# Rotary embedding on one core: loading the first tile as f32 on another queue, with compact constants and new rows

## The chip, the core and the metric

The kernel runs on one core of one Trainium2 chip. The metric is device time in microseconds (us), lower is better. A time in this text is the median of the runs of a kernel; the profile adds a span, which is about 2 us shorter than the time.

The data lies in HBM, the large memory; SBUF is the memory of the core, with 128 partitions. A transfer between them (DMA) is issued here by one of the engines SyncE, ScalarE and GpSimd, each with a queue of its own (136, 144 and 2304 packets in the kernel before), and carried in packets by the core's 16 DMA engines. VectorE and ScalarE compute on SBUF.

## The reference

```python
batch, n_heads, seq, head_dim = 8, 8, 1024, 64      # x is f32, 16.8 MB
angles = np.outer(positions, freqs)                 # 1024 x 32
cos, sin = np.cos(angles), np.sin(angles)
x_first, x_second = x[..., :32], x[..., 32:]
out_first  = x_first * cos - x_second * sin
out_second = x_first * sin + x_second * cos
```

The output is f32 and as large as the input. `positions` arrive as 64-bit integers.

## The kernel before

The 64 (batch, head) planes are cut into eight tiles of 128 partitions x 4096 elements. A partition holds 64 positions of one head, 16 KB of f32 in HBM. GpSimd issues all large transfers, and they cast: f32 in HBM, bf16 in SBUF, both ways. VectorE does six bf16 operations per tile.

```python
def hbm(t, g):                       # partition p takes row p of the tile: plain rows
    return bass.AP(tensor=t.tensor, offset=t.offset + g * P * run, ap=[[run, P], [1, run]])

pos_i = singles.tile([P, C, 1], positions.dtype)
nc.sync.dma_start(out=pos_i, in_=bass.AP(..., ap=[[0, group], [C, chunks], [1, C]]))
fr = singles.tile([P, half], f32)
nc.scalar.dma_start(out=fr, in_=freqs[None, :].to_broadcast([P, half]))
for g in range(ntiles):              # eight loads, f32 -> bf16
    nc.gpsimd.dma_start(out=xt..., in_=hbm(x, g))
# ... VectorE: turns = positions x freqs, range reduction; ScalarE: sin_h, cos_h (bf16)
for g in range(ntiles):
    v.tensor_mul(out=t1, in0=xf, in1=sin_h);  v.tensor_mul(out=t2, in0=xs, in1=sin_h)
    v.tensor_mul(out=of, in0=xf, in1=cos_h);  v.tensor_mul(out=os_, in0=xs, in1=cos_h)
    v.tensor_sub(out=of, in0=of, in1=t2);     v.tensor_add(out=os_, in0=os_, in1=t1)
    nc.gpsimd.dma_start(out=hbm(out, g), in_=ot...)      # store, bf16 -> f32
```

Of the kernel before, what the change touches and what calls it, by code (L numbers as in the profile page):

```python
# [2 lines left out]

# [4 lines left out]


@with_exitstack  # L10
def kernel(
    ctx: ExitStack,
    tc: tile.TileContext,
    x: bass.AP,
    freqs: bass.AP,
    positions: bass.AP,
    out: bass.AP,
):
    nc = tc.nc
    f32 = mybir.dt.float32  # L20
    bf16 = mybir.dt.bfloat16
    Sin = mybir.ActivationFunctionType.Sin
    Alu = mybir.AluOpType

    b, h, seq, d = x.shape
    bh = b * h
    half = d // 2
    P = 128
    twopi = 2 * math.pi


    C = 64
    chunks = seq // C
    group = P // chunks
    ntiles = bh // group
    run = C * d
    assert chunks * C == seq and group * chunks == P and ntiles * group == bh

    singles = ctx.enter_context(tc.tile_pool(name="singles", bufs=1))
    xpool = ctx.enter_context(tc.tile_pool(name="xin", bufs=ntiles))  # L40
    opool = ctx.enter_context(tc.tile_pool(name="xout", bufs=ntiles))
    tpool = ctx.enter_context(tc.tile_pool(name="tmp", bufs=2))

    def hbm(t, g):
        return bass.AP(tensor=t.tensor, offset=t.offset + g * P * run, ap=[[run, P], [1, run]])


    pos_i = singles.tile([P, C, 1], positions.dtype)
    nc.sync.dma_start(
        out=pos_i,  # L50
        in_=bass.AP(tensor=positions.tensor, offset=positions.offset,
                    ap=[[0, group], [C, chunks], [1, C]]))
    fr = singles.tile([P, half], f32)
    nc.scalar.dma_start(out=fr, in_=freqs[None, :].to_broadcast([P, half]))


    xts = []
    for g in range(ntiles):
        xt = xpool.tile([P, C, d], bf16)
        nc.gpsimd.dma_start(out=xt.rearrange("p c d -> p (c d)"), in_=hbm(x, g))  # L60
        xts.append(xt)


    half_pi = singles.tile([P, 1], f32)
    nc.vector.memset(half_pi, math.pi / 2)  # L65
    pos_f = singles.tile([P, C, 1], f32)
    nc.vector.tensor_copy(out=pos_f, in_=pos_i.bitcast(mybir.dt.int32)[:, :, :1])  # L67
    fturn = singles.tile([P, 1, half], f32)
    nc.vector.tensor_scalar_mul(out=fturn[:, 0, :], in0=fr, scalar1=1.0 / twopi)  # L69
    turns = singles.tile([P, C, half], f32)  # L70
    nc.vector.tensor_mul(out=turns, in0=pos_f.to_broadcast([P, C, half]),  # L71
                         in1=fturn.to_broadcast([P, C, half]))
    whole = singles.tile([P, C, half], f32)
    magic = 1.5 * 2.0 ** 23
    nc.vector.tensor_scalar(out=whole, in0=turns, scalar1=magic, scalar2=magic,  # L75
                            op0=Alu.add, op1=Alu.subtract)
    nc.vector.tensor_sub(out=turns, in0=turns, in1=whole)  # L77
    sin_h = singles.tile([P, C, half], bf16)
    cos_h = singles.tile([P, C, half], bf16)
    nc.scalar.activation(out=sin_h, in_=turns, func=Sin, scale=twopi)  # L80

    nc.scalar.activation(out=whole, in_=turns, func=mybir.ActivationFunctionType.Abs)  # L82
    nc.scalar.activation(out=cos_h, in_=whole, func=Sin, scale=-twopi, bias=half_pi)  # L83

    v = nc.vector
    for g in range(ntiles):
        xt = xts[g]
        xf = xt[:, :, :half]
        xs = xt[:, :, half:]
        ot = opool.tile([P, C, d], bf16)  # L90
        of = ot[:, :, :half]
        os_ = ot[:, :, half:]
        t1 = tpool.tile([P, C, half], bf16)
        t2 = tpool.tile([P, C, half], bf16)
        v.tensor_mul(out=t1, in0=xf, in1=sin_h)  # L95
        v.tensor_mul(out=t2, in0=xs, in1=sin_h)  # L96
        v.tensor_mul(out=of, in0=xf, in1=cos_h)  # L97
        v.tensor_mul(out=os_, in0=xs, in1=cos_h)  # L98
        v.tensor_sub(out=of, in0=of, in1=t2)  # L99
        v.tensor_add(out=os_, in0=os_, in1=t1)  # L100
        nc.gpsimd.dma_start(out=hbm(out, g), in_=ot.rearrange("p c d -> p (c d)"))  # L101


# [1 line left out]
_INS = ['x', 'freqs', 'positions']  # L105
_OUTS = [((8, 8, 1024, 64), 'float32')]


# [23 lines left out]
```

## Time and profile before

| | before |
|---|---|
| time | 86.48 us (86.31 to 86.53, 3 runs) |
| span of the profiled run | 84.2 us |
| first load packet starts / last store lands | 2.84 / 82.83 us |
| one tile's f32 side, load or store | 2.10 MB in 4.86 us, 431 GB/s |
| VectorE | 60.7 us busy, done at 67.7 us |

These are lines of the page of the kernel before: the span, the busy time of the engines, the busy tenths of VectorE and of the DMA engines in 40 slices of 2.1 us, what the DMA engines moved in each slice, and the DMA issues with KB and median us to landing.

```profile
span 84.2 us, 132 instructions
DVE 60.7 (72%) x54; ACT 7.0 (8%) x4; POOL 8.9 (11%) x20
DVE  0069927999999999999999999999999910000000
DMA  0399999999999999999999999999999999999990
GB/s 2 60 210 214 214 218 218 214 214 214 214 222 210 218 218 210 218 218 214 210 342 405 459 405 467 381 490 381 482 389 467 405 451 420 428 443 405 467 373 0
...
out_dram<-ot POOLq DMA_DIRECT2D x8, 2048.0 KB, 21.7
xt<-in_x_dram POOLq DMA_DIRECT2D x8, 1024.0 KB, 23.6
```

The DMA row is full from the third slice to the end: the kernel is a stream. The rate row counts the bytes written, so a cast load shows its bf16 side: 215 GB/s written means 430 GB/s read. Loads fill the first half and stores the second, because the stores queue behind the loads on one queue: the first store is issued at 22.6 us, and its first packet starts at 43.3 us, while the last packets of the loads end. VectorE is done when seven slices of stores are still to come.

The stages of the start, as windows (start:end, length, busy us of VectorE, ScalarE and GpSimd, TensorE clock, DMA share, GB/s written):

```profile
2.00:4.00 2.00, 0.00 (x0) 0.42 (x1) 2.00 (x5) 1.00 0.36 53
4.00:6.00 2.00, 1.04 (x3) 0.00 (x0) 1.63 (x4) 1.00 1.00 204
6.00:8.00 2.00, 1.97 (x2) 0.00 (x0) 0.00 (x0) 1.00 1.01 209
```

And from the timeline (start, duration, engine and line, what it did, in brackets what it waited for):

```profile
0.74 0.74 SPq L49 DMA_DIRECT2D pos_i<-in_positions_dram  x1
1.25 4.38 POOL L60 DMA_DIRECT2D xt<-in_x_dram  x8 [0.80 <-PEq L127]
4.93 0.20 DVE L67 CAST pos_f<-pos_i 128x64 f32<-128x64 int32 x1 [4.06 <-DMA pos_i<-in_positions_dram]
...
67.99 0.53 POOL L101 DMA_DIRECT2D out_dram<-ot  x1 [6.28 <-DVE ot L100]
```

The stream is thin until about 4.5 us. That head is what the change goes for. The last store is issued at 68.0 us, long before its turn on the queue.

### The profile page before, as it was taken

How to read it: one execution, taken by the hardware profiler on the slowest of the kernel's cores; microseconds unless marked ns; L12 is line 12 of the kernel's file. 1: busy time of each engine (PE TensorE's matmuls, PEld its weight loads, DVE VectorE, ACT ScalarE, POOL GpSimd, SP SyncE). 2: the span in 40 equal slices, each digit the busy share in tenths (PEclk: the TensorE clock that was granted, in tenths of full speed). 3: DMA queues.
4: the chain of work that ended last, by engine and by line, in shares of the span. 5: the costliest groups of instructions: out<-in, count | busy, mean ns of one | idle time of the engine just before them, and what ended most of it. 6: DMA issues, size and time to landing. Idle time of an engine off the chain costs nothing.

```text
span 84.2 us, 132 instructions
## 1 busy us (share of the span) xinstructions
DVE 60.7 (72%) x54; ACT 7.0 (8%) x4; POOL 8.9 (11%) x20
## 2 busy tenths in 40 slices
DVE  0069927999999999999999999999999910000000
ACT  4100079900000000000000000000000000000000
POOL 5960000000201100200200200100020020000000
DMA  0399999999999999999999999999999999999990
GB/s 2 60 210 214 214 218 218 214 214 214 214 222 210 218 218 210 218 218 214 210 342 405 459 405 467 381 490 381 482 389 467 405 451 420 428 443 405 467 373 0
DMA packets 2584, 25.25 MB, mean 300 GB/s; under 512 B 408, under 2 KB 536, under 8 KB 536
## 3 DMA queue, kind: packets, MB, share of 16 engines
q0 software_dynamic: 2304, 25.17, 97.2%
q1 hardware_dynamic: 136, 0.07, 0.3%
q10 hardware_dynamic: 144, 0.02, 0.1%
HBM read 16.86 MB, written 16.78 MB: 399 GB/s over the span
## 4 chain that ended last, share of the span: by engine, by line
issue 65%; DMA 10%; POOL 4%; POOLq 1%; PEldq 0%
DMA xt<-in_x_dram 10%; POOL out_dram L101 4%; POOLq L127 1%; POOLq L101 0%; PEldq L127 0%
## 5 line engine op out<-in xcount | busy, mean ns | idle before, releaser
L95 DVE TENSOR_TENSOR t<-xt,sin_h 128x2048 bf16<-128x2048 bf16 x8 | 9.8, 1224 | 2.0 <-ACT sin_h L80 2.0
L101 POOL DMA_DIRECT2D out_dram<-ot x8 | 4.3, 535 | 58.6 <-DVE ot L100 58.6
L99 DVE TENSOR_TENSOR ot<-ot,t 128x2048 bf16<-128x2048 bf16 x8 | 9.8, 1225 | 0.0
L97 DVE TENSOR_TENSOR ot<-xt,cos_h 128x2048 bf16<-128x2048 bf16 x8 | 9.8, 1224 | 0.0
L100 DVE TENSOR_TENSOR ot<-ot,t 128x2048 bf16<-128x2048 bf16 x8 | 9.8, 1224 | 0.0
L98 DVE TENSOR_TENSOR ot<-xt,cos_h 128x2048 bf16<-128x2048 bf16 x8 | 9.8, 1223 | 0.0
L96 DVE TENSOR_TENSOR t<-xt,sin_h 128x2048 bf16<-128x2048 bf16 x8 | 9.8, 1223 | 0.0
L60 POOL DMA_DIRECT2D xt<-in_x_dram x8 | 4.4, 578 | 0.8 <-PEq L127 0.8
L67 DVE CAST pos_f<-pos_i 128x64 f32<-128x64 int32 x1 | 0.2, 196 | 4.1 <-DMA pos_i<-in_positions_dram 4.1
L80 ACT ACTIVATE sin_h<-turns 128x2048 bf16<-128x2048 f32 x1 | 1.9, 1911 | 8.7 <-DVE turns L77 8.7
L77 DVE TENSOR_TENSOR turns<-turns,whole 128x2048 f32<-128x2048 f32 x1 | 2.3, 2293 | 0.0
L71 DVE TENSOR_TENSOR turns<-pos_f,fturn 128x2048 f32<-128x2048 f32 x1 | 2.3, 2291 | 0.0
L83 ACT ACTIVATE cos_h<-whole,half_pi 128x2048 bf16<-128x2048 f32 x1 | 2.0, 2003 | 0.0
L82 ACT ACTIVATE whole<-turns 128x2048 f32<-128x2048 f32 x1 | 1.9, 1896 | 0.0
L80 ACT ACT_TABLE_LOAD x1 | 1.3, 1283 | 1.1 <-PEq L116 1.1
L75 DVE TENSOR_SCALAR whole<-turns 128x2048 f32<-128x2048 f32 x1 | 1.2, 1226 | 0.0
L65 DVE MEMSET half_pi<- 128x1 f32 x1 | 0.1, 59 | 0.8 <-PEq L116 0.8
L69 DVE TENSOR_SCALAR fturn<-fr 128x32 f32<-128x32 f32 x1 | 0.2, 174 | 0.0
L116 POOL MEMSET const-float32-0.0<- 128x1 f32 x1 | 0.1, 99 | 0.2 <-issue 0.2
L116 POOL MEMSET const-bfloat16-1.0<- 128x1 bf16 x1 | 0.1, 102 | 0.0
L116 POOL MEMSET const-float32-1.0<- 128x1 f32 x1 | 0.1, 99 | 0.0
L116 POOL MEMSET const-uint8-127<- 128x1 uint8 x1 | 0.1, 99 | 0.0
## 6 DMA issues: line engine op xcount, KB each, us to landing
out_dram<-ot POOLq DMA_DIRECT2D x8, 2048.0 KB, 21.7
xt<-in_x_dram POOLq DMA_DIRECT2D x8, 1024.0 KB, 23.6
pos_i<-in_positions_dram SPq DMA_DIRECT2D x1, 64.0 KB
fr<-in_freqs_dram ACTq DMA_DIRECT2D x1, 16.0 KB, 3.6
```

Source lines behind the costliest of these rows:

```text
L60: nc.gpsimd.dma_start(out=xt.rearrange("p c d -> p (c d)"), in_=hbm(x, g))
L71: nc.vector.tensor_mul(out=turns, in0=pos_f.to_broadcast([P, C, half]), in1=fturn.to_broadcast([P, C, half]))
L77: nc.vector.tensor_sub(out=turns, in0=turns, in1=whole)
L80: nc.scalar.activation(out=sin_h, in_=turns, func=Sin, scale=twopi)
L83: nc.scalar.activation(out=cos_h, in_=whole, func=Sin, scale=-twopi, bias=half_pi)
L95: v.tensor_mul(out=t1, in0=xf, in1=sin_h)
L96: v.tensor_mul(out=t2, in0=xs, in1=sin_h)
L97: v.tensor_mul(out=of, in0=xf, in1=cos_h)
L98: v.tensor_mul(out=os_, in0=xs, in1=cos_h)
L99: v.tensor_sub(out=of, in0=of, in1=t2)
L100: v.tensor_add(out=os_, in0=os_, in1=t1)
L101: nc.gpsimd.dma_start(out=hbm(out, g), in_=ot.rearrange("p c d -> p (c d)"))
```

## The change

The intent: start the stream earlier. Tile 0 comes as f32 on SyncE's queue, which can issue at 0.74 us, and ScalarE casts it. So that the constants don't stand in the way, positions come on 16 partitions and frequencies on 4, and VectorE shuffles them within each group of 32 partitions. The rows are laid out anew, so that each group of 32 holds its own chunks of positions: partition = chunk x 8 + head. At the end SyncE waits early on all but the last store, to shorten the end.

```diff
     def hbm(t, g):
-        return bass.AP(..., ap=[[run, P], [1, run]])
+        return bass.AP(..., ap=[[run, chunks], [seq * d, group], [1, run]])
+    x0 = singles.tile([P, C, d], f32)
+    nc.sync.dma_start(out=x0.rearrange("p c d -> p (c d)"), in_=hbm(x, 0))
-    nc.sync.dma_start(out=pos_i, ...)
+    pos_i = singles.tile([P, C, words], i32)
+    nc.vector.memset(pos_i, 0)
+    nc.scalar.dma_start(out=pos_i[0:P:group].bitcast(positions.dtype),
+        in_=bass.AP(..., ap=[[C, chunks], [1, C], [1, 1]]))
     fr = singles.tile([P, half], f32)
-    nc.scalar.dma_start(out=fr, in_=freqs[None, :].to_broadcast([P, half]))
+    nc.vector.memset(fr, 0.0)
+    nc.scalar.dma_start(out=fr[0:P:32], in_=freqs[None, :].to_broadcast([P // 32, half]))
     for g in range(ntiles):
-        nc.gpsimd.dma_start(...)
+        if g:
+            nc.gpsimd.dma_start(...)
+    nc.vector.stream_shuffle(pos_i, pos_i, [i // group * group for i in range(32)])
+    nc.vector.stream_shuffle(fr, fr, [0] * 32)
 ... (sin_h and cos_h as before)
+    nc.scalar.copy(out=xts[0], in_=x0)
-    for g in range(ntiles):
+    for g in [1, 0] + list(range(2, ntiles)):
 ...
+    for done in [pos_i, fr, x0] + ots[:-1]:
+        sp.clobber_nop(outs=[sp.lower_ap(done)])
+    sp.keepalive_nop(ins=[sp.lower_ap(ots[-1])])
```

More of the change, by code (lines that the diff above doesn't have):

```diff
@@ L44, in hbm @@
     def hbm(t, g):
-        return bass.AP(tensor=t.tensor, offset=t.offset + g * P * run, ap=[[run, P], [1, run]])
-    pos_i = singles.tile([P, C, 1], positions.dtype)
-    nc.sync.dma_start(
-        out=pos_i,
+        return bass.AP(tensor=t.tensor, offset=t.offset + g * P * run,
+                       ap=[[run, chunks], [seq * d, group], [1, run]])
+    x0 = singles.tile([P, C, d], f32)
+    nc.sync.dma_start(out=x0.rearrange("p c d -> p (c d)"), in_=hbm(x, 0))
+    i32 = mybir.dt.int32
+    words = mybir.dt.size(positions.dtype) // 4
+    pos_i = singles.tile([P, C, words], i32)
+    nc.vector.memset(pos_i, 0)
+    nc.scalar.dma_start(
+        out=pos_i[0:P:group].bitcast(positions.dtype),
         in_=bass.AP(tensor=positions.tensor, offset=positions.offset,
-                    ap=[[0, group], [C, chunks], [1, C]]))
+                    ap=[[C, chunks], [1, C], [1, 1]]))
     fr = singles.tile([P, half], f32)
-    nc.scalar.dma_start(out=fr, in_=freqs[None, :].to_broadcast([P, half]))
+    nc.vector.memset(fr, 0.0)
+    nc.scalar.dma_start(out=fr[0:P:32], in_=freqs[None, :].to_broadcast([P // 32, half]))
     xts = []
@@ L59 @@
         xt = xpool.tile([P, C, d], bf16)
-        nc.gpsimd.dma_start(out=xt.rearrange("p c d -> p (c d)"), in_=hbm(x, g))
+        if g:
+            nc.gpsimd.dma_start(out=xt.rearrange("p c d -> p (c d)"), in_=hbm(x, g))
         xts.append(xt)
+    nc.vector.stream_shuffle(pos_i, pos_i, [i // group * group for i in range(32)])
+    nc.vector.stream_shuffle(fr, fr, [0] * 32)
     half_pi = singles.tile([P, 1], f32)
@@ L66 @@
     pos_f = singles.tile([P, C, 1], f32)
-    nc.vector.tensor_copy(out=pos_f, in_=pos_i.bitcast(mybir.dt.int32)[:, :, :1])
+    nc.vector.tensor_copy(out=pos_f, in_=pos_i[:, :, :1])
     fturn = singles.tile([P, 1, half], f32)
@@ L83 @@
     nc.scalar.activation(out=cos_h, in_=whole, func=Sin, scale=-twopi, bias=half_pi)
+    nc.scalar.copy(out=xts[0], in_=x0)
     v = nc.vector
-    for g in range(ntiles):
+    ots = []
+    for g in [1, 0] + list(range(2, ntiles)):
         xt = xts[g]
@@ L100 @@
         v.tensor_add(out=os_, in0=os_, in1=t1)
+        ots.append(ot)
         nc.gpsimd.dma_start(out=hbm(out, g), in_=ot.rearrange("p c d -> p (c d)"))
+    sp = nc.sync
+    for done in [pos_i, fr, x0] + ots[:-1]:
+        sp.clobber_nop(outs=[sp.lower_ap(done)])
+    sp.keepalive_nop(ins=[sp.lower_ap(ots[-1])])
 _INS = ['x', 'freqs', 'positions']
```

## The prediction

> **What bounds it now.** The DMA stream, from end to end. The row of DMA shares in 40 slices reads 9 from about 4.2 us to 82 us. Every tile is 2.10 MB on its f32 side. The semaphore arrivals in the trace space the eight load completions (9.8, 14.7, ... 43.9 us) and then the eight store completions (48.8, ... 82.8 us) by 4.86 us each: 431 GB/s of f32 side in both halves (the page's 215 GB/s for loads counts the bf16 side). 16 x 4.86 = 77.8 us, so of the span of 84.2 us only two ends are not stream: about 5.0 us before it (43.9 minus 8 x 4.86) and 1.4 us after it. [...] VectorE (60.7 us busy, 6.81 us per tile) is not the limit: it finishes at 67.7 us, the last store is issued at 68.0, but its packets start only at about 77.6, behind the older stores. That is some 8 us of slack.
>
> **What the change removes.** The empty head. GpSimd issues the first load at 1.25 us, its first packet starts at 2.8, and packets come one per 0.61 us on all engines only from about 4.5; the 264 small constant packets sit in front (1.7 to 4.6 us). In the new kernel SyncE can issue tile 0 at 0.74 us. ACT's constant load, issued at 0.74, had its first packet at 1.73; so I expect full rate from about 2.0 to 2.3 us, with GpSimd's stream joining before tile 0 runs out. The same bytes pass [...]. Gain: about 2.4 us, all on the critical path.
>
> **What it adds, off the path if the slack holds.** Two memsets and two shuffles (about 0.2 us each by the 0.2 us cast of the same partitions); positions now wait for a memset and travel beside 16 KB packets, landing perhaps 0 to 2 us later than 4.9; a ScalarE cast of 128x4096, about 3.8 us (twice the 1.9 us of 128x2048). VectorE may stall some 1.5 us for cos, as tile 0 is not there to fill in. VectorE then ends at about 69 to 72 us, while the last store's turn comes at about 75. Slack shrinks to 1 to 5 us but stays positive.
>
> **The tail.** After the last landing (82.83) SyncE makes four more waits to 83.10; pre-waiting saves about 0.2 us there. But GpSimd's drain ends only at 83.53 and the barrier follows it, so I count 0 to 0.2 us.
>
> **Risk.** The new layout puts one 16 KB run of eight heads on neighbouring partitions. If this changes which engine writes which partitions, or how reads spread in HBM, all 16 tiles may pay; 1% of the stream is 0.8 us.
>
> **Prediction.** 86.48 - 2.4 - 0.1 = 84.0 us; 8 in 10 between 83.2 and 85.6. Faster by over 2% (under 84.75): 0.72; within 2%: 0.23; slower by over 2%: 0.05.
>
> **What would show it.** The DMA row at 9 from the second slice of the span; last load completion at about 41.4 instead of 43.9; completion spacing still 4.86 us; last store landing at about 80.4; DMA share without a gap before the last store; VectorE's end at 69 to 72 us; GpSimd's last drain still ending about 0.7 us after the last landing.
>
> **What would make it wrong.** A spacing above 4.9 us (layout or f32 writes slow the stream); a gap before the last stores (VectorE late through constants or cast); tile 0's queue starting slowly, so that full rate comes no sooner than 4 us.

## The result and the profile after

The changed kernel took 87.79 us (87.65 to 88.13, 4 runs) against 86.44 us before (86.31 to 86.53, 4 runs). The ratio is 1.0163, 95% interval 1.0128 to 1.0198: slower by 1.6%, where a gain of 2.9% was forecast. Ratios here are the mean time of one kernel's runs over that of the other's runs in the same rounds, so not quite the ratio of the medians. Executions over 1.5% slower than the fastest of the same kernel are left out of the means. The profiled run was the slowest of the four (88.13 us).

The same lines of the page of the changed kernel:

```profile
span 86.4 us, 145 instructions
DVE 61.6 (71%) x60; ACT 10.5 (12%) x5; POOL 8.2 (9%) x19
DVE  0000239955579999999999999999999999940000
DMA  0998999999999999999999999999999999999970
GB/s 23 250 244 185 289 231 194 235 201 232 201 224 209 216 228 197 232 197 232 205 304 410 440 455 395 463 402 452 410 455 402 448 448 402 463 395 463 410 311 0
...
xt<-in_x_dram POOLq DMA_DIRECT2D x7, 1024.0 KB, 28.1
x<-in_x_dram SPq DMA_DIRECT2D x1, 2048.0 KB, 14.1
pos_i<-in_positions_dram ACTq DMA_DIRECT2D x1, 8.0 KB, 8.3
```

The DMA row is at 9 from the second slice, as forecast, and yet the kernel is slower. The row says how long the engines were busy, not how much they moved. In the second and third slices tile 0 goes f32 to f32, so 430 GB/s should be written there; it is 250 and 244. Tile 0 took 14.1 us from issue to landing. The same windows of the start:

```profile
2.00:4.00 2.00, 0.00 (x0) 1.28 (x1) 2.00 (x5) 1.00 1.20 295
4.00:6.00 2.00, 0.00 (x0) 0.01 (x1) 1.03 (x2) 1.00 1.03 213
6.00:8.00 2.00, 0.00 (x0) 0.00 (x0) 0.00 (x0) 1.00 0.81 184
```

From 4 to 6 us nothing but tile 0 moves: 213 GB/s at a share of 1.03. One of its 16 KB packets lasted 1.26 us there (median of 42), so 16 engines can bring 16 x 16384 B / 1.26 us = 208 GB/s. The timeline of the changed kernel:

```profile
0.74 0.62 SPq L51 DMA_DIRECT2D x<-in_x_dram  x1
1.03 0.60 ACTq L58 DMA_DIRECT2D pos_i<-in_positions_dram  x1
1.28 3.76 POOL L71 DMA_DIRECT2D xt<-in_x_dram  x7 [0.83 <-PEq L151]
1.67 1.02 ACTq L64 DMA_DIRECT2D fr<-in_freqs_dram  x1
9.45 0.01 DVE L74 LOAD_MASK_SELECT pos_i<-pos_i  x1 [8.40 <-DMA pos_i<-in_positions_dram]
12.14 0.01 DVE L75 LOAD_MASK_SELECT fr<-fr  x1 [2.15 <-DMA fr<-in_freqs_dram]
12.58 2.29 DVE L85 TENSOR_TENSOR turns<-pos_f,fturn 128x2048 f32<-128x2048 f32 x1
...
76.87 0.52 POOL L119 DMA_DIRECT2D out_dram<-ot  x1 [6.29 <-DVE ot L117]
```

Two more things show. The constants, though only 20 packets now (256 before; the prediction's 264 is a slip), reach VectorE at 9.4 and 12.1 us instead of 4.9. And GpSimd's first packet starts at 7.27 us in this trace, against 2.84 before, although it was issued at the same time. Both waited behind tile 0's packets: in the run without the f32 tile below (a4_no_f32_tile), with the same constants, the positions have landed by 3.5 us, the frequencies by 7.3 us, and GpSimd's first packet starts at 2.6 us.

To see where time is lost in a stream, one number is handy. Every packet of 8 KB or more stands for 16 KB of f32 side, and 431 GB/s is the rate of the kernel before. The lag at time t is t minus the time that the packets that had ended by then would need at that rate. It rises where the stream runs below its rate, and is flat where it runs at it. The whole stream is 16 tiles x 128 packets x 16384 B, 77.86 us, so the last packet ends at 77.86 us plus the last lag.

```
lag in us at t =         3     4     6    10    14    20    36    44    50    70    80   last packet ends
before                 3.00  4.00  4.63  4.68  4.69  4.72  4.68  4.81  4.84  4.88  4.62    82.46
after                  2.85  3.24  4.25  5.59  6.40  6.43  6.39  6.25  6.25  6.40  6.29    84.56
```

After the change the stream is ahead until about 6.5 us, but it loses from 3 us until 14 us, about as long as tile 0 is under way; from there it runs at full rate. All that has to be explained lies in the first 14 us, and 0.4 us in the very end (6.29 to 84.56 - 77.86 = 6.70): the 16 completions of the last store lie 1.39 us apart instead of 0.35.

### The profile page after: what moved, and what is told of

Same layout as the page of the kernel before. It is cut to its first block, busy times and chain, and to the rows that moved or that the text cites. A ratio compares the mean times of both kernels' runs of the same rounds, so it can differ in the third digit from the quotient of the medians.

```text
span 86.4 us, 145 instructions
## 1 busy us (share of the span) xinstructions
DVE 61.6 (71%) x60; ACT 10.5 (12%) x5; POOL 8.2 (9%) x19
## 4 chain that ended last, share of the span: by engine, by line
issue 79%; POOL 9%; POOLq 1%; PEldq 0%
POOL xt L71 4%; POOL out_dram L119 4%; POOLq L151 1%; POOLq L119 0%; PEldq L151 0%
## 5 line engine op out<-in xcount | busy, mean ns | idle before, releaser
L71 POOL DMA_DIRECT2D xt<-in_x_dram x7 | 3.8, 573 | 0.8 <-PEq L151 0.8
L99 ACT CAST xt<-x 128x4096 bf16<-128x4096 f32 x1 | 3.6, 3588 | 0.0
## 6 DMA issues: line engine op xcount, KB each, us to landing
x<-in_x_dram SPq DMA_DIRECT2D x1, 2048.0 KB, 14.1
```

Of the source, the lines that this page charges most:

```text
L71: nc.gpsimd.dma_start(out=xt.rearrange("p c d -> p (c d)"), in_=hbm(x, g))
L99: nc.scalar.copy(out=xts[0], in_=x0)
```

## The experiments

The theory (A): with the new rows, the partitions that are written at one time lie in steps of 8, and an f32 load into such partitions runs at half rate. Half of the rate is what the trace shows: 208 GB/s against 431. Which partitions are written together was my guess, as no trace names the engine or the partition of a packet. The rivals: (B) a copy of f32 to f32 on SyncE's queue is slow; (C) rows 256 KB apart in HBM are slow to read. Each run's lag stands at the end of this section.

### Plain rows for tile 0; the f32 load from GpSimd

```diff
-    nc.sync.dma_start(out=x0..., in_=hbm(x, 0))
+    nc.sync.dma_start(out=x0..., in_=bass.AP(..., ap=[[run, P], [1, run]]))   # a1_flat_rows
+    nc.gpsimd.dma_start(out=x0..., in_=hbm(x, 0))                             # a3_gpsimd_f32
```

> The changed kernel, but tile 0 is read into its partitions as plain rows (partition p takes row p of the tile) and not chunk by chunk over eight heads; its output is therefore wrong for tile 0, on purpose. Theory A [...]: with plain rows tile 0's packets take about 0.62 us instead of 1.24 us an engine, it lands by about 10 us instead of 14.8, the seventh cast load lands near 41 us instead of 45.7, and the time falls by 4 to 5 us to about 83.5. Theory B (a copy of f32 to f32 on SyncE's queue is slow by itself, whatever the rows): no change, about 87.8 us and 1.24 us a packet. Theory C (rows 256 KB apart in HBM are slow to read): as A.

> The changed kernel with the f32 load of tile 0 issued by GpSimd, ahead of its seven cast loads, rows as in the change; the result stays right. Theory A: still half rate, about 1.24 us a packet, tile 0 lands about 10 us after its first packet, and the time is 87 to 90 us. Theory B (the SyncE queue's copy is slow): 0.62 us a packet, tile 0 lands about 5.5 us after its first packet, time about 85. Theory C (HBM rows): the cast loads read the same rows at 4.8 us a tile in the changed kernel, so it expects about 0.62 us here too, unless it needs the first tile's time.

Plain rows: 85.69 us against 86.66 before, ratio 0.992 (0.987 to 0.996); output wrong for tile 0. Tile 0's packets take 0.62 us while it is alone (median of 57). The windows of this run:

```profile
2.00:4.00 2.00, 0.00 (x0) 1.28 (x1) 2.00 (x5) 1.00 0.65 229
4.00:6.00 2.00, 0.00 (x0) 0.01 (x1) 1.03 (x2) 1.00 1.00 383
6.00:8.00 2.00, 0.00 (x0) 0.00 (x0) 0.00 (x0) 1.00 1.07 325
```

From GpSimd: 89.54 us, ratio 1.033 (1.030 to 1.037), packets of 1.23 us (median of 106). So the queue is not the cause, and B falls. C is in trouble too, since cast loads of the same rows ran at full rate in the changed kernel (one each 4.87 us), but it is not yet out.

The time of the first run missed its forecast of 83.5 by over 2 us. Its trace shows two reasons. First, the start is worth less than I had thought: the first packets start at 1.74 us, but most of the first 16 take 1.1 to 1.9 us, and 229 GB/s is all that moves from 2 to 4 us; the lag is 3.1 at 4 us where I had reckoned with about 2.2. Second, a gap opens before the last store:

```profile
75.78 0.52 POOL L120 DMA_DIRECT2D out_dram<-ot  x1 [6.29 <-DVE ot L118]
```

```profile
76.00:77.00 1.00, 0.00 (x0) 0.00 (x0) 0.30 (x1) 1.00 0.60 229
```

The packets of the seventh store ran out from 75.9 us on (the DMA share is 0.60 from 76 to 77 us), and the first packet of the last store started only at 76.87 us. VectorE was late, because the frequencies had come at 11.0 us. In the changed kernel the same lateness was hidden, since its stream was later still: the last store was issued at 76.87 us, and its first packet started at 78.6 us.

### Tile 0 head by head

```diff
-    nc.sync.dma_start(out=x0..., in_=hbm(x, 0))
+    for e in [0, 1, 2, 3, 4, 5, 6, 7]:          # a5_heads_in_order
+    for e in [0, 4, 1, 5, 2, 6, 3, 7]:          # a6_heads_paired
+        nc.sync.dma_start(out=x0[e:P:group]..., in_=bass.AP(..., offset + e * seq * d,
+                          ap=[[run, chunks], [1, run]]))
```

> The changed kernel with tile 0's load cut into eight loads of 16 partitions, one for each head, in the order 0 to 7; same rows, same partitions, right result. Theory A: [...] tile 0 still runs near 1.2 us a packet and the time stays within 1 us of 87.8. A theory that blames the three-dimensional read pattern of one DMA expects 0.62 us a packet and about 84 us.

> As the one before, with the heads in the order 0, 4, 1, 5, 2, 6, 3, 7. [...] Theory A: [...] tile 0 runs clearly faster than in the order 0 to 7, between 0.62 and 0.9 us a packet, and the time is 2 to 4 us lower. If packets of an engine are written strictly one after the other and all engines stay in step, A expects no gain. Theories B and C: the order makes no difference.

In order: 87.96 us in the three fast runs (ratio 1.017, 1.014 to 1.021; a fourth run, 89.38 us, was slow). Paired: 88.28 us (1.020, 1.017 to 1.023). The packets took 1.10 and 1.14 us. Eight simple two-dimensional loads are as slow as the one load with three dimensions, so the shape of that access pattern is not the cause. The pairing gained nothing, where 2 to 4 us were forecast. The forecast rested on two packets of an engine in flight at a time; the traces don't show that: with tile 0 alone the changed kernel has 16 packets in flight most of the time and 18 at most, as many as there are engines. For packets one after the other the forecast itself expected no gain. So this tells less than I had hoped: in both runs the cast loads started at 2.8 us, so cast packets mixed with tile 0's, and which of them slowed each other can't be read from the trace. I count the pairing as inconclusive.

### Tile 0 by itself: partitions against HBM rows

To settle A against C, tile 0's f32 load runs alone here, as 16 loads of eight partitions; the cast loads are held back until it is in. The DMA share was about half (0.44 to 0.60 in the windows of 2 us from 4 to 14 us), so about eight of the 16 engines were at work at a time. The step between the partitions of one load is 8 or 4, and so is the step between the HBM rows. A1 is theory A for these loads; by A2 the packets to some groups of partitions are slow, whatever the step.

```diff
-    nc.sync.dma_start(out=x0..., in_=hbm(x, 0))
+    for e, r in groups:        # first partition and first row of each of the 16 loads
+        nc.sync.dma_start(out=x0[e:e + 7 * pstep + 1:pstep]...,
+            in_=bass.AP(..., offset + r * run, ap=[[rstep * run, 8], [1, run]]))
 ...
         if g:
+            nc.gpsimd.tensor_copy(out=xt[:, 0, :1], in_=x0[:, 0, :1])     # waits for tile 0
             nc.gpsimd.dma_start(...)
```

> Tile 0's f32 load measured by itself: 16 loads of 8 partitions with a step of 8 (0, 8, ... 56, then 64, 72, ... and so on), each plain rows, so that 8 engines work on it; the cast loads wait until tile 0 is in. Right rows are not kept, so tile 0's output is wrong on purpose. Theory A1 [...] a packet takes about 1.24 us an engine. Theory A2 [...]: here too most packets are slow, about 1.2 us.

> The same with 8 partitions in steps of 4 (0, 4, ... 28; 32, 36, ...; 64, ...; 96, ...). Theory A1: [...] packets take about 0.62 us an engine in all four groups, and tile 0 is in about twice as fast as with the step of 8. Theory A2: packets of the groups that start at 64 and 96, [...] stay at about 1.2 us, so half of the packets are slow. If both theories are wrong, step 4 and step 8 take the same.

> Tile 0's f32 load by itself again: 16 loads on partitions with a step of 8, now in an order [...] (0 to 7 as first partition, then 64 to 71), and reading the HBM rows that the step-4 run read. Output wrong for tile 0 on purpose. Theory A1 [...]: packets about 1.2 us, tile 0 takes about 19 us, more than the 14 us of the first step-8 run. If the HBM rows, not the partitions, made the difference between step 8 and step 4, packets are at 0.61 us as in the step-4 run.

> The counterpart: partitions in steps of 4, HBM rows in steps of 8. A1: about 0.61 us a packet, tile 0 in within about 12.5 us. If the HBM rows make the difference: 0.8 us or more a packet. The chip may limit the issue to one load per 0.66 us, so 0.61 us is the floor here.

These are single looks of unknown state (98.01, 96.34, 103.37 and 96.13 us, against 86.5 to 86.7 before; they are slow because the cast loads wait). Only the packets count. The median is over those that started after 4 us; the last column is when the last packet of tile 0 ended.

```
run               partition step  row step  order of the loads             packet us  tile 0 in at us
b1_step8                8             8     0, 64, 1, 65, ...                 0.79         16.2
b2_step4                4             4     0, 32, 64, 96, 1, ...             0.61         14.8
b3_step8_rows4          8             4     0, 1, ... 7, 64, ... 71           1.25         21.4
b4_step4_rows8          4             8     0, 1, 2, 3, 32, ...               0.61         14.3
```

Two forecasts missed: the first run's packets took 0.79 us and not 1.24, and the second run brought tile 0 in 12.5 us after its first packet against 14.0 in the first, not twice as fast. The third and the fourth run were planned after that. Their windows, with tile 0 alone on the engines:

```profile
6.00:8.00 2.00, 1.02 (x4) 0.00 (x0) 0.00 (x0) 1.00 0.52 123
12.00:14.00 2.00, 1.23 (x1) 0.74 (x1) 0.00 (x0) 1.00 0.58 123
```

```profile
6.00:8.00 2.00, 2.00 (x1) 0.00 (x0) 0.00 (x0) 1.00 0.48 197
12.00:14.00 2.00, 0.00 (x0) 2.00 (x2) 0.00 (x0) 1.00 0.46 188
```

The step of the partitions decides: of two runs whose loads read the same rows, the one with a step of 8 is the slower (third against second: 1.25 and 0.61 us; first against fourth: 0.79 and 0.61). With partitions in steps of 4 the rows make no difference (0.61 twice). Rows 256 KB apart were not tried here, but cast loads of such rows run at full rate (the run with the new rows alone, below): C falls. With a step of 8, eight engines with packets of 1.25 us bring 8 x 16384 B / 1.25 us = 105 GB/s, and the third run's whole tile, 2.10 MB in 19.2 us, makes 109. In the fourth run the packets take no longer than with plain rows (0.61 us, 215 GB/s while busy); what holds it up is SyncE, which issues a load each 0.67 us (16 in 10.79 us). The first run lies between (0.79 us). It differs from the third in order and rows together, and the alternating order of a6_heads_paired gained nothing, so the reason is not shown. A2 falls too: in the second run, with loads on all four groups of partitions, 10 of 108 packets took over 1 us, where half should have been slow. Why partitions in steps of 8 are slow no run shows.

What remains an inference is the step from here to the changed kernel: the trace doesn't name the engine or the partition of a packet, so that the packets under way there at one time lie in steps of 8, too, is concluded from the same packet time (1.26 and 1.25 us) and from the cure by plain rows (0.62 us), not read off.

### What the other parts are worth

```diff
a4_no_f32_tile:      the changed kernel without x0; all eight tiles as cast loads, in order
e1_no_f32_no_waits:  the same, without SyncE's early waits
d1_new_rows_only:    the kernel before with the new rows; positions as [[C, chunks], [0, group], [1, C]]
a7_no_sync_waits:    the changed kernel without the clobber_nop and keepalive_nop lines
```

> The changed kernel without its f32 tile: all eight tiles come as cast loads from GpSimd, in order; the constants on few partitions, the shuffles, the new rows and SyncE's early waits stay. Theory (the loss is all in the f32 load; the cast loads run at full rate with the new rows): packets of the first tile start near 2.8 us as in the kernel before, but without the 264 constant packets in front the stream is full from about 3.5 us, so it ends 0.8 to 1.6 us earlier than the kernel before: 84.9 to 85.7 us. Constants land by about 4 us, VectorE ends by 68 us. Rival (the new rows or the shuffles cost by themselves): 86.5 us or more.

> The run without the f32 tile, also without SyncE's early waits, so that against the run with the new rows alone only the constants differ. If the early waits slowed the middle of that stream, its loss of 1.5 us between 20 and 44 us is gone and the time is about 85.2. If the loss comes from engines that run closely in step over the new rows (the completions of a load lay only 0.3 us apart there, 0.6 us with the new rows alone), it stays: about 86.6 us.

> The kernel before with only its rows changed to those of the change (all eight tiles as cast loads, positions replicated by their load). [...] the load half of the stream loses 0.5 to 1.5 us, as in the run without the f32 tile, time 87.0 to 88.0. If the rows are harmless to cast loads: 86.4 or, [...] up to 0.5 us less.

> The changed kernel without SyncE's early waits at its end. The trace puts GpSimd's drain 0.69 us (before) and 0.66 us (after) behind the last landing, later than SyncE in both; so the waits should be worth nothing: same time as the changed kernel, within 0.2 us, and 1.4 us from last landing to the end of the span. If the early waits did shorten the end, this run is 0.2 us slower.

- Without the f32 tile: 86.59 us, ratio 1.002 (0.998 to 1.005). The stream is 1.0 us ahead of the kernel before at 10 us (lag 3.65 against 4.68), as expected, but it loses all of that by 44 us, and the forecast of 84.9 to 85.7 missed.
- Also without the early waits: 86.56 us, ratio 1.001 (1.000 to 1.003). The lag is flat until 36 us, then 1.2 us are lost between 36 and 44 us, in the packets of the last load, which last up to 1.34 us. So the waits are not the cause of that loss.
- New rows alone: 86.25 us, ratio 0.998 (0.995 to 1.002), no loss. My forecast of 87 or more, for new rows that slow the cast loads, missed: cast loads, which write half of the bytes (1024 KB a tile, not 2048), lose nothing with the new rows. The new rows alone are not the cause of the loss at 40 us either.
- Without the early waits: 87.98 us on a chip whose runs of the kernel before gave 86.42, ratio 1.0175 against the changed kernel's 1.0163, within the intervals of both. From the last landing to the end of the span it is 1.41 us before, 1.40 after and 1.39 in this run. The first barrier of the end waits for GpSimd's drain, which ends 0.66 to 0.70 us after the last landing in all three, while SyncE is through 0.14 us after it with the early waits and 0.27 and 0.39 us without.

The loss at 40 us, small in some runs and over 1 us in these two, stays open. In the kernel before, too, a few packets of the last load last up to 0.96 us at 41 to 42 us; in the changed kernel none do. The completions of a load lie 0.3 us apart in a4_no_f32_tile and 0.6 us with the new rows alone; whether the loss has to do with that, no run isolates.

### Versions that combine the findings

All three keep plain rows, load the positions on 32 partitions without a memset (partition 2c + r has chunk c) and spread them over the four groups of 32 with VectorE.

```diff
+    pos_q = singles.tile([32, C, words], mybir.dt.int32)
+    nc.scalar.dma_start(out=pos_q.bitcast(positions.dtype),
+        in_=bass.AP(..., ap=[[C, chunks], [0, 2], [1, C], [1, 1]]))
+    fr = singles.tile([32, half], f32)
+    nc.sync.dma_start(out=fr, ...)       # c1 (ahead of tile 0), c2;  c3: nc.gpsimd, tile 0 is first on nc.sync
+    nc.vector.tensor_copy(out=pos_q_f, in_=pos_q[:, :, 0])
+    for q in range(0, P, 32):
+        nc.vector.stream_shuffle(pos_f[q:q + 32, :, 0], pos_q_f, [2 * (i % 16) for i in range(32)])
+        nc.vector.tensor_scalar_mul(out=fturn[q:q + 32, 0, :], in0=fr, scalar1=1.0 / twopi)
```

> A combination: plain rows for all tiles as in the kernel before; tile 0 as f32 on SyncE's queue with ScalarE's cast; positions on 32 partitions and frequencies on 32, loaded without a memset and issued ahead of tile 0, then spread over the four quadrants by VectorE; none of SyncE's early waits. Theory A and the late constants as second cause: tile 0 at about 0.62 us a packet, constants landed by 5 us, VectorE done by 71 us, no gap before the last store, all loads in by about 41.5 to 42.5 us, time 84.0 to 85.0 us. If something else in the f32 path costs, 85.5 or more as with plain rows alone.

> As the one before, without the f32 tile: the kernel before with only its constants changed (32 partitions, spread by VectorE). Theory: the same gain as the run without the f32 tile, 0.8 to 1.6 us against the kernel before, 84.9 to 85.7 us. The difference to the combination is what the early f32 tile is worth by itself once it runs at full rate: 0 to 1 us.

> Plain rows; tile 0 as f32 the first thing on SyncE's queue; positions on 32 partitions first on ACT's queue; frequencies on 32 partitions first on GpSimd's queue, ahead of its cast loads; the rest as in the combination before. The run with plain rows alone had only 3.1 us of stream lost at 5 us against 3.8 in the combination, so I expect 0.6 us less than that: 85.0 to 85.5 us, constants in by 9 us, VectorE done before 74 us, no gap before the last store. If the constants land after 10 us, the gap is back and it is 85.7 or more.

- c1_early_f32_plain: 85.94 us against 86.42, ratio 0.994 (0.990 to 0.999). Tile 0 waited for the frequencies on its queue, and its first packet started at 2.28 us, not 1.74. There is no gap before the last store, which was issued at 69.8 us. The forecast of 84 to 85 missed.
- c2_few_constants_plain, all cast loads: 85.96 us, ratio 0.994 (0.990 to 0.998). The forecast of 84.9 to 85.7 missed. Against c1 the f32 tile is worth nothing here, where it isn't first.
- c3_f32_first: 85.18 us (85.03 to 85.38) against 86.45, ratio 0.985 (0.982 to 0.989), the best of all, and the forecast was right. It beats both kernels. Constants are in by 8.1 us. Of its profile:

```profile
span 83.3 us, 144 instructions
DMA  4799999999999999999999999999999999999970
GB/s 86 259 407 334 240 193 224 216 204 232 201 240 193 224 216 204 232 201 232 189 397 448 417 464 405 432 440 409 448 417 464 409 440 432 409 456 409 464 307 0
...
x<-in_x_dram SPq DMA_DIRECT2D x1, 2048.0 KB, 9.1
```

```profile
76.00:77.00 1.00, 0.00 (x0) 0.00 (x0) 0.00 (x0) 1.00 1.22 492
```

The third slice writes 407 GB/s, where the changed kernel wrote 244; tile 0 lands 9.1 us after its issue instead of 14.1; and the gap at 76 us is gone.

The lags of all runs but those with tile 0 by itself:

```
lag in us at t =         3     4     6    10    14    20    36    44    50    70    80   last packet ends
before                 3.00  4.00  4.63  4.68  4.69  4.72  4.68  4.81  4.84  4.88  4.62    82.46
after                  2.85  3.24  4.25  5.59  6.40  6.43  6.39  6.25  6.25  6.40  6.29    84.56
a7_no_sync_waits       3.00  3.35  4.18  5.44  5.79  5.71  5.89  5.79  5.86  5.86  5.75    84.06
a1_flat_rows           2.81  3.13  3.15  3.50  3.70  3.62  3.57  3.59  3.59  3.67  4.54    82.14
a3_gpsimd_f32          3.00  3.51  4.71  6.35  7.65  7.61  7.60  7.62  7.58  7.62  7.66    85.47
a5_heads_in_order      2.85  2.90  3.53  4.37  5.45  6.62  6.81  6.71  6.70  6.78  6.79    84.84
a6_heads_paired        2.81  2.97  3.26  3.99  5.37  6.77  6.62  6.59  6.55  6.67  6.75    84.68
a4_no_f32_tile         3.00  3.47  3.57  3.65  3.66  3.62  4.37  5.11  5.03  5.00  5.15    83.20
e1_no_f32_no_waits     3.00  3.43  3.57  3.50  3.70  3.62  3.76  4.96  4.99  4.96  4.88    82.97
d1_new_rows_only       3.00  4.00  4.21  4.22  4.27  4.26  4.26  4.39  4.42  4.39  4.31    82.25
c2_few_constants_plain 3.00  3.81  4.02  3.99  4.12  4.03  3.95  4.47  4.46  4.39  4.47    82.53
c1_early_f32_plain     3.00  3.66  3.76  3.88  3.77  3.77  3.84  4.20  4.16  4.16  4.20    82.46
c3_f32_first           2.89  3.28  3.22  3.31  3.32  3.43  3.19  3.48  3.43  3.55  3.52    81.57
```

## Why the prediction was wrong

- **What bounds the kernel** was right: the stream, at 431 GB/s of f32 side, before and after. The store spacing stayed near 4.86 us.
- **"I expect full rate from about 2.0 to 2.3 us"** is the step that failed, in two ways. The larger: tile 0 did start at 2.14 us, but at half rate. The prediction assumed that the same bytes take the same time on another queue, and priced the new layout only as 1% of the whole stream. It is a loss of the f32 tile alone: the lag at 14 us is 6.40 us in the changed kernel and 3.70 us with tile 0 in plain rows, so 2.7 us (2.1 us in the faster execution without the early waits, a7_no_sync_waits, whose lag is 5.79). The cause is which SBUF partitions are written at one time, shown with tile 0 by itself (1.25 us a packet in steps of 8 against 0.61 in steps of 4, from the same HBM rows). That the layout brings the changed kernel into this pattern is inferred.
- **The size of the gain** was also too large. With plain rows the lag at 6 us is 3.15 us against 4.63 before, so 1.5 us, not 2.4, because the first packets are slow (most of the first 16 took 1.1 to 1.9 us; why, no run shows); by 14 us it is 1.0 us. The best version gained 1.3 us of time.
- **The sum** in the trace: from a lag of 4.69 us at 14 us, 1.0 us of gain and 2.7 us of half rate give 6.4; the uneven end of the last store adds 0.4. The last packet ends at 84.56 us instead of 82.46, and the span is 2.1 us longer. The timed medians differ by less, 1.35 us, as the profiled run was the slowest.
- **"Slack shrinks to 1 to 5 us but stays positive"** held in the changed kernel, but the constants were mis-sized: "perhaps 0 to 2 us later than 4.9" became 4.5 us for the positions and 7.2 us for the frequencies (9.4 and 12.1 us). VectorE ended at 76.6 us, not at 69 to 72. With tile 0 at full rate this would have bound: the plain-row run has a gap before its last store, and the lag jumps there from 3.67 to 4.54.
- **The tail, "0 to 0.2 us"**, is 0: GpSimd's drain ends last, 0.66 us after the last landing, with SyncE through at 0.14 us.
- **"A spacing above 4.9 us (layout or f32 writes slow the stream)"** named the right suspect among what could go wrong, but expected it in all tiles and gave it little weight.

## What to carry to other kernels

When a transfer is cast no longer, its SBUF side doubles (tile 0: from 1024 to 2048 KB): check the rate of both sides, and which partitions are written at the same time (1.25 us a packet in steps of 8, 0.61 in steps of 4). Full busy marks of the DMA engines don't show this (9 in the third slice of the changed kernel); the bytes moved per slice (244 GB/s there, 407 in c3_f32_first), and the time of one packet (1.26 us, not 0.62), do. Small loads that a long chain waits for came late behind a large one: the positions landed at 9.3 us in the changed kernel and at 3.6 us in c1_early_f32_plain, issued ahead of tile 0. But to put them first is a choice: the best version, c3_f32_first, lets the large load go first, has its constants at 8.1 us, and that was early enough for VectorE. And the gain of an early start should be taken from the lag of a stream that has really begun early.

## What the runs measured besides

- A small load beside a large one on another queue: 16 packets of positions, issued at 1.03 us beside 16 KB packets of 1.26 us, started only at 6.0 to 7.2 us and had landed at 9.3 us; issued ahead of tile 0 (c1_early_f32_plain), 32 packets had landed by 3.6 us. The memset that they wait for is not the cause: without it, but issued together with tile 0 (c3_f32_first), they landed at 8.0 us; with it, but with tile 0's load issued by GpSimd (a3_gpsimd_f32), 2.5 us after their issue.
- An f32 load of all 128 partitions whose DRAM side has three dimensions, 16 outermost: its packets took 1.26 us instead of 0.62, and it ran at 208 GB/s instead of 431. That the partitions written at one time are the cause is inferred (see above).
- GpSimd's drain after the last of its own stores, for which the end of the kernel waits: it ended 0.66 to 0.70 us after the last landing.
- The slow start of a stream: with plain rows most of the first 16 packets of 16 KB took 1.1 to 1.9 us against 0.62 later; the first started at 1.74 us, and the lag was 3.1 us at 4 us, so some 1.4 us of stream were lost.
